# A two-layer hybrid encoder trunk on one Trainium2 core: the one-pass matrix products run their columns from the last to the first

## The chip, the core and the metric

The kernel runs on one core of one Trainium2 chip. The metric is the device time of one launch in microseconds (us), lower being better; a kernel's time is the median of its runs. TensorE does the matrix products (PE in the profile, and PEld for the loading of its stationary operand), VectorE is DVE, ScalarE is ACT, GpSimd is POOL, and SyncE (SP) issues most of the DMAs.

## The reference

Two layers over 512 tokens of width 1024. Layer 0 mixes the tokens by differential attention, layer 1 by chunk-causal gated linear attention; both also attend to 256 memory tokens, and each ends in a gated MLP with a causal convolution of width 3. Cut to what matters:

```python
for i in range(2):
    h = rms_norm(x, attn_norm[i])
    if i == 0:
        proj = h @ w_in_diff[0]                 # 512x1024 @ 1024x2560
        mix = diff_attention(q, k, v, ...)      # 6 heads, two maps of width 64 each
    else:
        proj = h @ w_in_gla[0]                  # 512x1024 @ 1024x2576
        mix = gla_attention(q, k, v, r, ...)    # 4 heads, chunks of 64
    cross = memory_cross_attention(mem_q, mem, mem_norm[i], w_mem_kv[i], mem_qk_norm[i])
    x = x + concatenate([mix, cross], -1) @ w_out[i]      # 512x1024 @ 1024x1024
    h = rms_norm(x, ffn_norm[i])
    u = h @ w_up[i]                             # 512x1024 @ 1024x5632
    a, g = split(causal_conv3(u) + conv_b[i])
    x = x + (silu(g) * a) @ w_down[i]           # 512x2816 @ 2816x1024
```

All inputs and outputs are float32.

## The kernel before

**A product in three one-pass terms.** TensorE takes operands of a rounded type (fp32r in the profile) in one pass. The kernel splits each float32 operand of a large product into a rounded high part and a rounded rest (`hi` and `lo`), and forms `hi*hi + hi*lo + lo*hi`: three matmuls, each with a stationary operand of 128x128 and a moving operand of 128 rows, added up in the same bank of PSUM. These are the one-pass products. A bank holds 512 float32 columns, and the moving operand and the output of a one-pass product are 512, 272 or 256 columns wide. The smaller products (the attention's scores and values, the transposes, the sums of squares) are of plain float32; each of them is recorded as two matmuls.

**Where they are issued.** There are four places.
- `gemm` (L327 to L329): the projections. The stationary operand is a block of 128 tokens of the activations, the moving one a row of weights; one bank collects eight row blocks of three terms.
- `product` (L348 to L350): the output projection and the MLP's up-projection. Here the weights are stationary and the activations (512 tokens) move.
- L507: the very first projection, written out by hand so that it starts while the inputs still arrive.
- `step` in `down` (L1173): the MLP's down-projection, done by a scheme of seven products of halves for each of its two column halves; the moving operand is 256 tokens wide, and two outputs of 256 columns share a bank.

One further pair of lines makes rounded products, the gates of layer 1 (L885); the change leaves it alone.

**What sets the order.** TensorE's instructions stand in the order in which they are written out. A queue of small pieces of work, `Filler`, holds the large products of the projections, and the attention code lets it run for so many microseconds between its own steps (`F.fill`), so that TensorE has products to do while VectorE and ScalarE work on a softmax. The banks come from a pool with two buffers for each of four names (`mm`, `sm`, `lg`, `tp`). Semaphore waits between the engines, and of an engine on itself, are put in by the framework from the regions that the instructions read and write.

**Who reads the banks.** ScalarE or VectorE takes a finished bank out, in ascending column order, once its last product has ended: L1178 for the down-projection, L1064 for the output projection, ScalarE's copies for the projections.

Of the kernel before, what the change touches and what calls it, by code (L numbers as in the profile page):

```python
# [22 lines left out]
KT = D // 128  # L23
# [127 lines left out]
def trunk(ctx, tc, head_d, x_t, mem_t, wpack, cols_a_d, cols_d, conv_d, gate_d, rel_bias, diff_lambda, consts, onehot, out):  # L151
    nc = tc.nc
    mm = nc.tensor.matmul
# [10 lines left out]
    def bank(tag):  # L164
        return ps.tile([128, 512], F32, name=f"ps_{tag}", tag=tag)

    def xtile():
        return xs.tile([128, S], F32, name="xt", tag="xs", bufs=XS)

    def pair(dt=F32):  # L170
        t = xs.tile([128, 2, S], dt, name="x2", tag="x2", bufs=X2)
        return t[:, 0], t[:, 1]
# [10 lines left out]
    def blk(b, w=128):  # L183
        return slice(w * b, w * b + w)
# [6 lines left out]
    eps = perm.tile([128, 1], F32, name="eps")  # L191
    V.memset(eps, EPS)

    def transpose(dst, src):
        n = src.shape[0]
        nc.tensor.transpose(dst, src, ident[:n, :n])  # L196
# [35 lines left out]
    def raw_tile():  # L232
        return wp.tile([128, WTILE], F32, name="raw", tag="raw", bufs=RAWS)

    def load_raw(raw, n):
        nc.sync.dma_start(raw[:, :n], wpack[at[0], :, :n])
        at[0] += 1
        return raw
# [57 lines left out]
    def weights(key, more=True):  # L296
        i = used[0]
        assert plan[i][0] == key, (plan[i][0], key)
        if more:
            prefetch(i)  # L300
        used[0] += 1
        parts, made[i] = made[i], None
        return parts
# [10 lines left out]
    def gemm(sh, sl, nb, key, w, evac, hook=None, order=None, hold=1):  # L314
        got, open_, held = [], {}, []
        order = order or [(b, "mm") for b in range(nb)]

        def unit(b, tag, k0, k1):
            if not got:
                for x in key if isinstance(key, list) else [key]:  # L320
                    got.extend(weights(x))
            if k0 == 0:
                open_[b] = bank(tag)[:, :w]
            p = open_[b]
            for k in range(k0, k1):
                hi, lo = got[k]
                mm(p, sh[k][:, blk(b)], hi, start=k == 0, stop=False)  # L327
                mm(p, sh[k][:, blk(b)], lo, start=False, stop=False)  # L328
                mm(p, sl[k][:, blk(b)], hi, start=False, stop=k == KT - 1)  # L329
            if k1 == KT:  # L330
                held.append(b)
                if len(held) < hold:
                    return
                if hook is not None and order[hold - 1][0] == b:
                    hook()
                for x in [x for x in held if x in open_]:
                    evac(x, open_.pop(x))
        for b, tag in order:
            for k in range(0, KT, 2):
                F.add(6 * w / 2370.0, lambda b=b, tag=tag, k=k: unit(b, tag, k, k + 2))  # L340


    def product(p, parts, n, pairs, ids=None):
        ids = range(len(parts)) if ids is None else ids
        first, last = (ids[0], ids[-1]) if len(ids) == len(parts) else (0, len(parts) - 1)
        for i in ids:
            (hi, lo), (bh, bl) = parts[i], pairs[i]
            mm(p, hi[:, blk(n)], bh, start=i == first, stop=False)  # L348
            mm(p, hi[:, blk(n)], bl, start=False, stop=False)  # L349
            mm(p, lo[:, blk(n)], bh, start=False, stop=i == last)  # L350


    xT, xpair = [None] * KT, [None] * (KT // 2)
# [56 lines left out]
    first = [bank("mm"), bank("mm"), bank("sm"), bank("sm")]  # L410
# [24 lines left out]
    with tc.tile_pool(name="ini", bufs=1) as ip, tc.manual_schedule(engines={E.Activation, E.DVE, E.Pool, E.SP}):  # L435
        idle = ip.tile([128, 512], F32, name="idle")
        rb = ip.tile([32, 6], F32, name="rb")
        oh = ip.tile([32, 640], F32, name="oh")
        bs = pair()
        bs = bs[0][:6], bs[1][:6, :128]  # L440
        lv = xtile()[:, :256]
        G.memset(idle, 0.0)
        p = bank("tp")
        for n in (512, 320):
            mm(p[:, :n], idle[:, 0:128], idle[:, :n], start=True, stop=True)


        raws = [ip.tile([128, WTILE], F32, name=f"raw{i}") for i in range(4)]
        A.dma_start(raws[0][:, blk(0, S)], wpack[0, :, blk(0, S)])
        head = ip.tile([128, 32 + S], F32, name="head")  # L450
        for c in (slice(0, 32 + S // 2), slice(32 + S // 2, 32 + S)):
            load(head[:, c], head_d[:, c])
        xT[0] = head[:, 32:]
        for k in range(1, KT):
            if k % 2:
                two = pair()
            xT[k] = two[1 - k % 2]
            load(xT[k], x_t[k])
            load(raws[k // 2][:, blk(k % 2, S)], wpack[k // 2, :, blk(k % 2, S)])
        load(cols_a, cols_a_d)  # L460
        at[0] = 4
        load(C[:, 640:768], consts[:, 640:768])
        load(rb, rel_bias)
        load(oh, onehot)
        second = [load_raw(raw_tile(), WTILE) for _ in range(3)]
        load(cols, cols_d)
        load(lv, diff_lambda[0].rearrange("a b -> (a b)").partition_broadcast(128))
        parts, acc, split_w = [], [None], [None]
        made.append(parts)

        def operands(k):
            if k % 2 == 0:
                split_w[0] = [wp.tile([128, WTILE], F32R, name=n, tag=n, bufs=WB) for n in ("whi", "wlo")]
            c = blk(k % 2, S)
            hi, lo = split_w[0]
            xh[k], xl[k] = split_tiles()
            if k == 0:
                V.tensor_copy(hi[:, c], raws[0][:, c])
                V.tensor_sub(lo[:, c], raws[0][:, c], hi[:, c].bitcast(F32))
                for t in (blk(0, S // 2), blk(1, S // 2)):  # L480
                    split(xh[0][:, t], xl[0][:, t], xT[0][:, t], col(0, head))
            else:
                split(xh[k], xl[k], xT[k], col(k, head))
                split_weights(c, raws[k // 2], hi, lo)
            parts.append((hi[:, c], lo[:, c]))
            squares(xT[k], acc)

        operands(0)
        for k in range(KT):
            if k + 1 < KT:  # L490
                operands(k + 1)
            if k == 0:
                second.append(load_raw(raws[0], WTILE))
            if k == 4:
                bias_rows(rb, oh, bs)
            if k == KT - 2:
                make_piece(second, lambda: token_rsqrt("lg", acc[0], NB, r_x[:, 0]))
                weights(("qk", 0))
                small_vectors()
                for c in range(2):  # L500
                    load(bias_d[:, 512 * c:min(512 * c + 512, 640)], bs[c])
            hi, lo = parts[k]
            terms = (xh[k], hi), (xh[k], lo), (xl[k], hi)
            todo = [(b, i) for b in range(NB) for i in range(3)]
            for b, i in sorted(todo, key=lambda bi: bi[1]) if k == 0 else todo:
                xp, w = terms[i]
                mm(first[b], xp[:, blk(b)], w, start=k == 0 and i == 0, stop=k == KT - 1 and i == 2)  # L507

    load(C[:, 0:640], consts[:, 0:640])
    for i in range(4):  # L510
# [595 lines left out]
    def ffn(pool, l, acc):  # L1106
# [47 lines left out]
        def down(g, mids, finish):  # L1154
            last, ks = len(mids) - 1, tuple(range(len(mids)))
            parts, banks, first, last_group = {}, {}, used[0], g + 1 == len(GROUPS)

            def step(c, tag, w, m, ks=ks, start=False, more=True):
                if (c, w) not in parts:
                    parts[c, w] = weights(("d", l, g, c, w), more)  # L1160
                elif more:
                    prefetch(first + more)
                if start:
                    banks[c, tag] = bank(tag)
                p = banks[c, tag]
                hi, lo = parts[c, w]
                for k in ks:
                    mh, ml = mids[k][m]
                    for n in range(2):
                        o, ws = p[:, blk(n, 256)], slice(256 * k + 128 * n, 256 * k + 128 * n + 128)  # L1170
                        terms = (hi, mh), (hi, ml), (lo, mh)
                        for i, (a, b) in enumerate(terms):
                            mm(o, a[:, ws], b, start=start and (k, n, i) == (0, 0, 0), stop=k == last and i == 2,  # L1173
                               skip_group_check=True)

            def add(c, tag, f, t):
# [89 lines left out]
        for what, i in _ffn():  # L1266
            if what == "up":
# [12 lines left out]
                if i % 2 == 0:  # L1280
                    w = pool.tile([128, 8, 256], F32, name="w", bufs=1)
# [3 lines left out]
            else:  # L1285
                n, last = GROUPS[i], i == len(GROUPS) - 1
# [93 lines left out]
```

## Time and profile before

| | |
|---|---|
| median of 3 runs | 1177.33 us (1175.06 to 1177.44) |
| the profiled execution | 1175.44 us |
| its span, first to last instruction | 1173.7 us |
| granted TensorE clock | 1.00 |
| PE busy | 1156.1 us, 6448 records |
| PEld busy | 988.8 us |
| DVE busy | 887.9 us |
| ACT busy | 599.1 us |
| POOL busy | 4.1 us |
| DMA | 117.94 MB, 100 GB/s |

"Busy" counts a stretch once however many instructions overlap in it. TensorE's matmuls overlap: the next one starts before the last columns of the one before have come out, so a matmul's own duration is longer than the distance to the next one's start. The pace of a chain is read from those distances in the timeline, and the duration minus the distance is the overlap.

### The profile page before, as it was taken

The numbers are of one execution on the slowest core, as the hardware profiler recorded it, in microseconds if no ns is written. First come the engines' busy times: TensorE is split into PE (matmuls) and PEld (weight loads), VectorE is DVE, ScalarE is ACT, GpSimd is POOL, SyncE is SP. The second block draws the span as 40 slices with busy tenths as digits, with TensorE's granted clock in tenths as the row PEclk, the third lists the DMA queues.
The fourth block names the chain that finished last, engine by engine and source line by source line (L and its number), as shares of the span: only waits on it lengthen the run. The fifth ranks groups of instructions, "written<-read, shape, count | busy, mean of one in ns | idle before, by whom it ended". The sixth has DMA issues, their size and how long they took to land.

```text
span 1173.7 us, 16700 instructions
## 1 busy us (share of the span) xinstructions
PE 1156.1 (99%) x6448; PEld 988.8 (84%) x6448; DVE 887.9 (76%) x1454; ACT 599.1 (51%) x1048; POOL 4.1 (0%) x17
## 2 busy tenths in 40 slices
PE   9999999999999999999999999999999999999998
PEld 6877776788899889988997788988789988998888
DVE  7747677779986778668897736868998777876885
ACT  6856676556444444344467534436654344434441
POOL 0000000000000000000000000000000000000000
PEclk9999999999999999999999999999999999999999
DMA  9532213243126222532253221144322632253211
GB/s 306 164 100 90 68 55 109 76 114 104 62 70 190 90 72 73 162 92 70 65 172 108 72 73 46 46 161 126 86 68 64 184 103 73 72 158 95 72 37 73
DMA packets 39277, 117.94 MB, mean 100 GB/s; under 512 B 4671, under 2 KB 6520, under 8 KB 39198
## 3 DMA queue, kind: packets, MB, share of 16 engines
q1 hardware_dynamic: 39054, 116.62, 31.8%
q8 instruction: 51, 0.84, 0.3%
q10 hardware_dynamic: 144, 0.26, 0.1%
q14 instruction: 28, 0.23, 0.1%
HBM read 112.65 MB, written 4.21 MB: 100 GB/s over the span
## 4 chain that ended last, share of the span: by engine, by line
PE 89%; DVE 6%; ACT 2%; DMA 1%; issue 1%; SPq 0%; DVEq 0%; ACTq 0%
PE ps_lg L1173 10%; PE ps_mm L349 8%; PE ps_mm L350 8%; PE ps_mm L348 8%; PE ps_sm L350 7%; PE ps_sm L349 7%; PE ps_sm L348 7%; PE ps_mm L327 5%; PE ps_mm L329 5%; PE ps_mm L328 5%; PE ps_tp L1173 5%; PE ps_mm L1173 3%; PE ps_tp L196 2%; PE ps_lg L686 1%; PE ps_sm L722 1%
## 5 line engine op out<-in xcount | busy, mean ns | idle before, releaser
L230 DVE TENSOR_TENSOR wlo<-raw,whi 128x1024 fp32r<-128x1024 f32 (+4 forms) x164 | 186.7, 1141 | 86.5 <-ACT whi L227 85.7
L227 ACT CAST whi<-raw 128x1024 fp32r<-128x1024 f32 (+4 forms) x164 | 160.7, 985 | 154.3 <-PE ps_sm L349 69.7
L348 PE MATMUL ps_mm<-x,whi 128*128 128x512 f32 x438 | 172.6, 394 | 0.4 <-DVE midh L1262 0.4
L349 PE MATMUL ps_mm<-x,whi 128*128 128x512 f32 x438 | 170.6, 389 | 0.2 <-DVE x L309 0.2
L350 PE MATMUL ps_mm<-x,wlo 128*128 128x512 f32 x438 | 170.6, 390 | 0.0
L348 PE MATMUL ps_sm<-x,whi 128*128 128x512 f32 x378 | 148.0, 392 | 0.0
L349 PE MATMUL ps_sm<-x,whi 128*128 128x512 f32 x378 | 147.1, 389 | 0.0
L350 PE MATMUL ps_sm<-x,wlo 128*128 128x512 f32 x378 | 147.1, 389 | 0.0
L327 PE MATMUL ps_mm<-whi,x 128*128 128x512 f32 (+2 forms) x336 | 132.0, 393 | 0.0
L329 PE MATMUL ps_mm<-whi,x 128*128 128x512 f32 (+2 forms) x336 | 126.6, 377 | 0.5 <-DVE x L309 0.4
L328 PE MATMUL ps_mm<-wlo,x 128*128 128x512 f32 (+2 forms) x336 | 126.1, 375 | 0.0
L263 ACT CAST whi<-raw 128x1024 fp32r<-128x1024 f32 (+1 forms) x60 | 58.3, 978 | 86.8 <-PE ps_sm L349 26.2
L348 PEld LDWEIGHTS ps_mm<-x,whi 128*128 128x128 f32 x438 | 82.2, 188 | 17.3 <-issue 0.9
L350 PEld LDWEIGHTS ps_mm<-x,wlo 128*128 128x128 f32 x438 | 82.2, 188 | 17.1
L349 PEld LDWEIGHTS ps_mm<-x,whi 128*128 128x128 f32 x438 | 82.3, 188 | 17.0 <-DVE x L309 0.6
L265 DVE TENSOR_TENSOR wlo<-raw,whi 128x1024 fp32r<-128x1024 f32 (+1 forms) x60 | 67.9, 1132 | 25.1 <-ACT whi L263 25.0
L349 PEld LDWEIGHTS ps_sm<-x,whi 128*128 128x128 f32 x378 | 71.0, 188 | 15.0 <-issue 0.5
L348 PEld LDWEIGHTS ps_sm<-x,whi 128*128 128x128 f32 x378 | 71.0, 188 | 15.0 <-issue 0.5
L350 PEld LDWEIGHTS ps_sm<-x,wlo 128*128 128x128 f32 x378 | 70.9, 188 | 14.7
L1173 PE MATMUL ps_lg<-midh,whi 128*128 128x256 f32 x264 | 74.9, 284 | 1.8 <-DVE x L1178 1.8
L1173 PE MATMUL ps_lg<-midh,wlo 128*128 128x256 f32 x264 | 74.7, 283 | 0.0
L1173 PE MATMUL ps_lg<-midl,whi 128*128 128x256 f32 x264 | 74.7, 283 | 0.0
(308 smaller groups left out, 2288.5 us busy)
## 6 DMA issues: line engine op xcount, KB each, us to landing
raw<-in_wpack_dram SPq DMA_DIRECT2D x170, 512.0 KB, 3.6
raw<-in_wpack_dram SPq DMA_DIRECT2D x24, 384.0 KB, 3.1
x<-in_x_t_dram SPq DMA_DIRECT2D x15, 256.0 KB, 4.1
xres<-x SPq DMA_DIRECT2D x8, 256.0 KB, 3.9
x<-xres SPq DMA_DIRECT2D x8, 256.0 KB, 4.7
out_dram<-x SPq DMA_DIRECT2D x8, 256.0 KB, 2.2
raw<-in_wpack_dram SPq DMA_DIRECT2D x7, 256.0 KB, 5.5
bt<-bias_d SPq DMA_DIRECT2D x6, 256.0 KB, 4.9
```

The lines of the kernel that those rows point to most:

```text
L196: nc.tensor.transpose(dst, src, ident[:n, :n])
L227: ins = A.copy(hi[:, c], raw[:, c])
L230: V.tensor_sub(lo[:, c], raw[:, c], hi[:, c].bitcast(F32))
L263: A.copy(hi[:, c], raw[:, c])
L265: todo = [lambda: V.tensor_sub(lo[:, c], raw[:, c], hi[:, c].bitcast(F32)), lambda: [sum_weights((*key[:3], *x)) for x in after]]
L327: mm(p, sh[k][:, blk(b)], hi, start=k == 0, stop=False)
L328: mm(p, sh[k][:, blk(b)], lo, start=False, stop=False)
L329: mm(p, sl[k][:, blk(b)], hi, start=False, stop=k == KT - 1)
L348: mm(p, hi[:, blk(n)], bh, start=i == first, stop=False)
L349: mm(p, hi[:, blk(n)], bl, start=False, stop=False)
L350: mm(p, lo[:, blk(n)], bh, start=False, stop=i == last)
L1173: mm(o, a[:, ws], b, start=start and (k, n, i) == (0, 0, 0), stop=k == last and i == 2, skip_group_check=True)
```

## The change

At all four places the moving operand and the output are given through a view with a step of -1: TensorE reads the moving operand's last column first and writes the output's last column first. The same numbers end in the same places. The stationary operands, the readers of the banks, the float32 products and the gates of layer 1 are as they were.

```diff
+    def back(t):
+        return t[:, ::-1]
+
...
-                mm(p, sh[k][:, blk(b)], hi, start=k == 0, stop=False)
-                mm(p, sh[k][:, blk(b)], lo, start=False, stop=False)
-                mm(p, sl[k][:, blk(b)], hi, start=False, stop=k == KT - 1)
+                mm(back(p), sh[k][:, blk(b)], back(hi), start=k == 0, stop=False)
+                mm(back(p), sh[k][:, blk(b)], back(lo), start=False, stop=False)
+                mm(back(p), sl[k][:, blk(b)], back(hi), start=False, stop=k == KT - 1)
...
-            mm(p, hi[:, blk(n)], bh, start=i == first, stop=False)
-            mm(p, hi[:, blk(n)], bl, start=False, stop=False)
-            mm(p, lo[:, blk(n)], bh, start=False, stop=i == last)
+            mm(back(p), hi[:, blk(n)], back(bh), start=i == first, stop=False)
+            mm(back(p), hi[:, blk(n)], back(bl), start=False, stop=False)
+            mm(back(p), lo[:, blk(n)], back(bh), start=False, stop=i == last)
...
-                mm(first[b], xp[:, blk(b)], w, start=k == 0 and i == 0, stop=k == KT - 1 and i == 2)
+                mm(back(first[b]), xp[:, blk(b)], back(w), start=k == 0 and i == 0, stop=k == KT - 1 and i == 2)
...
-                            mm(o, a[:, ws], b, start=start and (k, n, i) == (0, 0, 0), stop=k == last and i == 2,
+                            mm(back(o), a[:, ws], back(b), start=start and (k, n, i) == (0, 0, 0), stop=k == last and i == 2,
                                skip_group_check=True)
```

On every engine the instructions and their order stay the same. What moves is a number of waits of TensorE on its own semaphore (PE_49 below): 23 matmuls, each the first of its bank, have such a wait now and had none, and 7 that had one have none. One place is where the output projection of layer 0 opens a bank during the attention (`x_1240` is a half of the rounded mix of heads, `em` the attention's weights). Before:

```order
776 L722 MATMUL ps_sm<-v_388,em 128x128 x3
777 L348 MATMUL ps_mm<-x_1240,whi 128x512
778 L349 MATMUL ps_mm<-x_1240,whi 128x512
779 L350 MATMUL ps_mm<-x_1240,wlo 128x512
780 L196 MATMUL ps_tp<-C,em 128x128 [waits DVE_49,PE_49]
```

And now, with the lines three further down in the file:

```order
776 L725 MATMUL ps_sm<-v_388,em 128x128 x3
777 L351 MATMUL ps_mm<-x_1240,whi 128x512 [waits PE_49]
778 L352 MATMUL ps_mm<-x_1240,whi 128x512
779 L353 MATMUL ps_mm<-x_1240,wlo 128x512
780 L199 MATMUL ps_tp<-C,em 128x128 [waits DVE_49,PE_49]
```

The first product into the bank has gained the wait; the two that follow it into the same bank have none, and no instruction has changed its place.

## The prediction

> **What bounds the kernel now.** I read the page's busy rows first, then the waits of TensorE, then the chain, then the pace of the products in the timeline.
>
> ```profile
> PE 1156.1 (99%) x6448; PEld 988.8 (84%) x6448; DVE 887.9 (76%) x1454; ACT 599.1 (51%) x1048; POOL 4.1 (0%) x17
> PEclk9999999999999999999999999999999999999999
> PE 89%; DVE 6%; ACT 2%; DMA 1%; issue 1%; SPq 0%; DVEq 0%; ACTq 0%
> PE ps_tp L196 <- DVE qm L388: 2.8, 1, 2.8
> ```
>
> TensorE is busy in all but 17.6 us of a span of 1173.7 us (1173.7 - 1156.1), at its full clock in every slice; its longest single wait for another engine is 2.8 us. The chain that ended last is TensorE's work for 89%. So the time is the number of TensorE's products times the pace at which they follow each other, plus little. DVE, the next busiest, has 285 us of slack. Nothing that the change does reaches the other engines except through the moment at which a bank is finished.
>
> A busy TensorE need not run at its peak, so the pace itself is read from the timeline (start, duration, line). First the 512-wide one-pass products of `product`, 18 steps apart, then the 256-wide ones of the down-projection, 6 steps apart.
>
> ```profile
> 244.93 0.39 PE L348 MATMUL ps_mm<-mxh,whi 128*128 128x512 f32 x1
> ...
> 249.01 0.39 PE L348 MATMUL ps_mm<-x,whi 128*128 128x512 f32 x1
> ```
> ```profile
> 471.68 0.28 PE L1173 MATMUL ps_lg<-midh,whi 128*128 128x256 f32 x1
> ...
> 472.40 0.28 PE L1173 MATMUL ps_lg<-midh,whi 128*128 128x256 f32 x1
> ```
>
> 4.08 us over 18 steps is 226.7 ns for 512 columns; 0.72 us over 6 is 120.0 ns for 256. The difference, 106.7 ns for 256 columns, is 0.417 ns for a column, and what is left is a fixed part of 13.3 ns at either width. Each product lasts 0.39 us (or 0.28), so 163 ns of it overlap the next one (0.39 - 0.227, 0.28 - 0.12).
>
> How many there are comes from the busy time by source line (busy, count, for PE and then PEld; one row each for L348, L327, L507 and L1173) and from the groups that keep shapes apart.
>
> ```profile
> 0.00:1174.00 1174.00, 326.80 (x832) 156.23 (x832) 1.00 0.32 100
> 0.00:1174.00 1174.00, 136.66 (x352) 66.29 (x352) 1.00 0.32 100
> 0.00:1174.00 1174.00, 22.83 (x96) 18.00 (x96) 1.00 0.32 100
> 0.00:1174.00 1174.00, 223.35 (x1848) 222.68 (x1848) 1.00 0.32 100
> ```
> ```profile
> L327 PE MATMUL ps_mm<-whi,x 128*128 128x512 f32 x288 | 117.8, 409 | 0.0
> L327 PE MATMUL ps_mm<-whi,x 128*128 128x256 f32 x32 | 9.6, 301 | 0.0
> ```
>
> L348 has 832, and so have L349 and L350: 2496, all 512 wide. L327 to L329 have 3 x 352 = 1056: 864 of 512, 96 of 256, and the other 96 are 272 wide. L507 adds 96 of 512. So 3456 are 512 wide, and 1848 + 192 = 2040 are 256 or (96 of them) 272 wide; I count the latter as 256. At the paces above they fill 3456 x 226.7 ns + 2040 x 120 ns = 783 + 245 = 1028 us, 88% of the span. The change touches every one of these 5496, and nothing hides a nanosecond of them.
>
> **The change part by part.** The instructions and their order stay; three things could have a price.
>
> *Reading the moving operand backwards.* No TensorE row of before reads or writes with a negative step. The nearest row that reads backwards is VectorE's L691, which takes the attention's bias table with a step of -1; beside it stands a forward read of the same size:
>
> ```profile
> L691 DVE CUSTOM_DVE_ANT_0 em<-ps_lg,bt 128x512 f32<-128x512 f32 x12 | 8.0, 688 | 5.4 <-PE ps_lg L686 5.1 <-PE ps_sm L722 0.3
> L1178 DVE TENSOR_TENSOR x<-x,ps_lg 128x512 f32<-128x512 f32 x48 | 32.8, 684 | 10.0 <-PE ps_lg L1173 10.0
> ```
>
> 688 ns against 684 ns: backwards costs VectorE nothing. But it takes 1.34 ns for a column (688/512), while a one-pass product needs one every 0.417 ns, three times as fast. The row shows that the step is handled, not that it is handled at TensorE's one-pass pace.
>
> *Writing the output backwards.* Here there is not even a distant row: every writer of before goes upwards. What the trace does show is a slower pace at which the same TensorE reads and writes the same columns, the plain float32 products:
>
> ```profile
> 262.61 1.02 PE L1127 MATMUL ps_tp<-xt,C 128*128 128x512 f32 x2
> 702.82 1.14 PE L983 MATMUL ps_lg<-gv,kd 128*96 128x192 f32 x6
> ```
> ```profile
> L1127 PE MATMUL ps_tp<-xt,C x4: 592/592/593, 262.6 to 821.9; 128*128 128x512 f32 x4
> L983 PE MATMUL ps_lg<-gv,kd x24: 325/326/326, 702.8 to 774.9; 128*96 128x192 f32 x24
> ```
>
> Two 512-wide ones take 1.02 us and each lasts 592 ns, so they are 428 ns apart; six 192-wide ones take 1.14 us, so they are (1140 - 326)/5 = 163 ns apart. That is 0.83 ns for a column, twice 0.417, with a fixed part of about 3 ns. So TensorE has a full and a half pace for columns of four bytes, and a one-pass product runs at the full one. My estimate is that the full pace needs neighbouring columns to be taken and put two at a time in ascending order, and that a step of -1 drops the product to the half pace of these rows.
>
> The price of that: a 512-wide product goes from 226.7 to 512 x 0.834 + 3 = 430 ns if the fixed part falls to that of the float32 rows, and to 440 ns if it stays 13.3; a 256-wide one goes from 120 to 216.5 or 226.8 ns. By the first, 3456 x 203.3 ns + 2040 x 96.5 ns = 702.6 + 196.9 = 899.5 us; by the second, 3456 x 213.6 + 2040 x 106.8 = 738.2 + 217.9 = 956.1 us. Nothing in the rows tells which, so I take the middle, 928 us. The bounds of this part are nothing (L691) and 956 us, with more only in the last rival below; for a gain I see a reason only in the rival that names it.
>
> [...]
>
> *The new waits.* 23 first products of a bank now wait on TensorE's own semaphore. The dearest case is that a wait is for the product just ahead, which loses the overlap of 163 ns: 23 x 0.163 = 3.7 us. The cheapest is nothing: the framework adds a wait for the bank's former products, and those ended before ScalarE or VectorE emptied the bank, for which the new first product waits as it is. TensorE has some 55 such waits already, and none of them stands among its waits in the trace of before, whose longest entries are for other engines. I take nothing, and keep 0 to 3.7 us; the 7 waits that go are worth nothing either. While it waits, all of TensorE's queue stands behind it, and nobody else.
>
> The sum, against the profiled execution (1175.4 us, its span and 1.7 us around it; 0.16% below the median of the runs): 1175.4 + 928 + 0 = 2103 us. All of it lies on TensorE, which works in order. VectorE's 888 us and ScalarE's 599 us would spread over 2100 us and bind nowhere new; at most they shorten some of TensorE's 17.6 us of idle time. For this case alone the range is 1175.4 + 899.5 - 17.6 = 2057 to 1175.4 + 956.1 + 3.7 = 2135, rounded to 2055 to 2140.
>
> **The rivals.**
>
> *Direction is free.* [...] For it: L691 is as fast backwards as forwards, all rows start at a multiple of four columns and have an even width, so descending pairs are the same pairs as ascending ones. Against it: L691 is at a third of the pace. Then only the new waits are left: 1175.4 to 1179.1 us, not slower than can be told from no change, and this is the case on the other side of the forecast. It decides where the product keeps its 227 ns. With what runs differ by, 1173 to 1180. Chance 0.25.
>
> *A price for each product, not each column.* The start of a backward product costs more, at the fixed part of 13.3 ns or in the overlap of 163 ns. Another fixed part is 5496 x 13.3 ns = 73 us, so 1248 us; the loss of the whole overlap (the next product held until the former's columns are all in) is 5496 x 163 ns = 896 us, so 2071 us. For it: products into one bank follow each other column by column, and a check of that could know ascending order only. Against it: both products run in the same direction, so each column still has the same time between its two writes. Chance 0.14, anywhere between 1248 and 2071.
>
> *A gain.* The fixed part of 13.3 ns could come from the jump from the last column back to the first, and shrink to the 3 ns of the float32 rows: 5496 x 10.3 ns = 57 us, so 1119 us. Against it: a descending product jumps just as far, the other way, and the float32 rows jump too. Chance 0.07.
>
> *A quarter of the pace.* Each column is fetched alone and costs two of the half-pace steps, 1.67 ns: 3456 x 640 ns + 2040 x 320 ns = 2865 us more, 4040 us. No row of TensorE is that slow. Chance 0.07.
>
> **How the numbers follow.** The half pace has the remaining 0.47 and gives the time, 2103 us; its own range is 2055 to 2140. The range over the cases must hold 8 in 10: with the free direction (0.25), the price for each product (0.14) and the half pace (0.47) it holds 0.86, from 1173 to 2140; leaving out the free direction would leave out 0.39. About 0.2% (2.4 us) is what a measurement of this kernel can tell from no change. Within it lies the free direction but for 0.02 above (the waits at their dearest) and 0.01 below: same 0.22. Faster is the gain and that 0.01: 0.08. Slower is the rest: 0.70.
>
> **What would show each step.** In the profile of the changed kernel I look at the distance between starts of one-pass products: about 430 to 440 ns at 512 columns and 216 to 227 ns at 256 under the forecast, PE busy near 2080 us, durations up from 0.39 to about 0.6 us, and DVE's share of the span near 42%. The gates' products (L885, now L888), which stay forward and rounded, keep their durations. If the distances stay 227 and 120 ns, the step from slower rows to a backward one was wrong and direction is free. If the distances grow by the same amount at both widths, it is a price for each product: by 13 ns with durations as they were, or to the whole duration of 0.39 and 0.28 us. If only matmuls that open a bank show idle time ahead of them, with TensorE as its releaser, the waits cost what I took as nothing.

## The result and the profile after

| | before | after |
|---|---|---|
| median of 4 runs | 1177.38 us (1175.06 to 1177.49) | 1193.88 us (1192.13 to 1194.72) |
| ratio, 95% interval | | 1.0147 [1.0134, 1.0159] |
| the profiled execution | 1175.44 us | 1192.13 us |

The change costs 1.5%: far more than can be mistaken for no change, and less than a fiftieth of what was forecast. From the page of after (its span, the busy rows of the engines, the granted clock, the chain that ended last) and from TensorE's waits (for whom, us in all, times, longest):

```profile
span 1190.3 us, 16706 instructions
PE 1173.2 (99%) x6448; PEld 986.7 (83%) x6448; DVE 888.2 (75%) x1454; ACT 598.7 (50%) x1048; POOL 4.1 (0%) x17
PEclk9999999999999999999999999999999999999999
PE 88%; DVE 7%; ACT 2%; issue 1%; DMA 0%; DVEq 0%; ACTq 0%
PE ps_tp L199 <- DVE qm L391: 2.7, 1, 2.7
```

TensorE is busy for 17.1 us more (1173.2 - 1156.1) and the span is 16.6 us longer (1190.3 - 1173.7). The other engines do what they did, the granted clock stands in the top tenth in every slice (0.999 in the mean), and TensorE's longest wait is the one of before. So the time went into TensorE's own pace. The timeline of after shows it (start, duration): 18 steps of `product`, then 6 steps of the down-projection.

```profile
247.94 0.40 PE L351 MATMUL ps_mm<-x,whi 128*128 128x512 f32 x1
...
252.14 0.40 PE L351 MATMUL ps_mm<-x,whi 128*128 128x512 f32 x1
```
```profile
478.60 0.28 PE L1176 MATMUL ps_lg<-midh,whi 128*128 128x256 f32 x1
...
479.31 0.28 PE L1176 MATMUL ps_lg<-midh,whi 128*128 128x256 f32 x1
```

4.20 us over 18 steps is 233.3 ns, where before had 226.7: 6.6 ns more for each 512-wide product. 0.71 us over 6 is 118 ns, where before had 120: the 256-wide ones are a little faster. The busy time by source line (busy, count, for PE and then PEld; L351, then L1176) says the same of whole lines: 326.80 us became 333.44, and 223.35 became 220.77.

```profile
0.00:1191.00 1191.00, 333.44 (x832) 156.47 (x832) 1.00 0.32 99
0.00:1191.00 1191.00, 220.77 (x1848) 219.95 (x1848) 1.00 0.32 99
```

Adding up, over all TensorE's records of a place, the distance from each matmul's start to the next one's start gives the account of the whole change (worked out from the start times in the traces, us):

| place | records | before | after | read alone | write alone | 32 bytes before the weights |
|---|---|---|---|---|---|---|
| `product` | 2496 | 570.8 | 586.4 | 586.4 | 570.8 | 586.0 |
| `gemm` | 1056 | 233.4 | 236.8 | 237.5 | 233.7 | 236.6 |
| L507 | 96 | 23.0 | 22.8 | 23.3 | 23.8 | 23.2 |
| down step | 1848 | 224.0 | 222.0 | 221.9 | 224.0 | 223.4 |
| all else | 952 | 116.2 | 116.2 | 117.1 | 117.3 | 117.1 |

From before to after that is 15.6 + 3.4 - 0.2 - 2.0 = 16.8 us, all of the longer span. `product` pays 15.56 us / 2496 = 6.2 ns a matmul. (The entries are rounded; unrounded, the distances grow by 16.7 us and the span, 1173.65 to 1190.35 us, by 16.7 too.) The last three columns belong to experiments below.

### The profile page after: what moved, and what is told of

Read it like the earlier page. It is cut to its first block, busy times and chain, and to the rows that moved or that the text cites. A ratio compares the mean times of both kernels' runs of the same rounds, so it can differ in the third digit from the quotient of the medians.

```text
span 1190.3 us, 16706 instructions
## 1 busy us (share of the span) xinstructions
PE 1173.2 (99%) x6448; PEld 986.7 (83%) x6448; DVE 888.2 (75%) x1454; ACT 598.7 (50%) x1048; POOL 4.1 (0%) x17
## 4 chain that ended last, share of the span: by engine, by line
PE 88%; DVE 7%; ACT 2%; issue 1%; DMA 0%; DVEq 0%; ACTq 0%
PE ps_lg L1176 9%; PE ps_mm L352 8%; PE ps_mm L351 8%; PE ps_mm L353 8%; PE ps_sm L352 8%; PE ps_sm L353 8%; PE ps_sm L351 8%; PE ps_mm L330 5%; PE ps_mm L331 5%; PE ps_mm L332 5%; PE ps_tp L1176 4%; PE ps_mm L1176 2%; PE ps_tp L199 2%; PE ps_lg L689 1%; DVE wlo L268 1%
## 5 line engine op out<-in xcount | busy, mean ns | idle before, releaser
L351 PE MATMUL ps_mm<-x,whi 128*128 128x512 f32 x438 | 176.0, 402 | 0.1
L352 PE MATMUL ps_mm<-x,whi 128*128 128x512 f32 x438 | 174.2, 398 | 0.2 <-DVE x L312 0.2
L353 PE MATMUL ps_mm<-x,wlo 128*128 128x512 f32 x438 | 174.1, 397 | 0.0
L351 PE MATMUL ps_sm<-x,whi 128*128 128x512 f32 x378 | 151.1, 400 | 0.0
L353 PE MATMUL ps_sm<-x,wlo 128*128 128x512 f32 x378 | 150.2, 397 | 0.0
L352 PE MATMUL ps_sm<-x,whi 128*128 128x512 f32 x378 | 150.2, 397 | 0.0
L330 PE MATMUL ps_mm<-whi,x 128*128 128x512 f32 (+2 forms) x336 | 133.6, 398 | 0.0
L332 PE MATMUL ps_mm<-whi,x 128*128 128x512 f32 (+2 forms) x336 | 128.2, 382 | 0.5 <-DVE x L312 0.4
L351 PEld LDWEIGHTS ps_mm<-x,whi 128*128 128x128 f32 x438 | 82.4, 188 | 19.5 <-issue 0.6
L351 PEld LDWEIGHTS ps_sm<-x,whi 128*128 128x128 f32 x378 | 71.1, 188 | 17.2 <-issue 0.5
L1176 PE MATMUL ps_lg<-midh,whi 128*128 128x256 f32 x264 | 74.8, 284 | 2.3 <-DVE x L1181 2.3
L330 PEld LDWEIGHTS ps_mm<-whi,x 128*128 128x128 f32 x336 | 63.3, 188 | 14.4 <-issue 3.3
L332 PEld LDWEIGHTS ps_mm<-whi,x 128*128 128x128 f32 x336 | 63.2, 188 | 14.1 <-DVE x L312 1.0
```

What stands on the lines that cost most here:

```text
L330: mm(back(p), sh[k][:, blk(b)], back(hi), start=k == 0, stop=False)
L332: mm(back(p), sl[k][:, blk(b)], back(hi), start=False, stop=k == KT - 1)
L351: mm(back(p), hi[:, blk(n)], back(bh), start=i == first, stop=False)
L352: mm(back(p), hi[:, blk(n)], back(bl), start=False, stop=False)
L353: mm(back(p), lo[:, blk(n)], back(bh), start=False, stop=i == last)
L1176: mm(back(o), a[:, ws], back(b), start=start and (k, n, i) == (0, 0, 0), stop=k == last and i == 2, skip_group_check=True)
```

## The experiments

**The pace by itself.** The trunk is left out; chains of 48 one-pass products run into a bank, each with fresh weights, forward and backward, at several widths.

```python
def cols(t, w, how, o=0):
    if how == "b":
        return t[:, o:o + w][:, ::-1]
    if how == "s":
        return t[:, o:o + 2 * w:2]
    return t[:, o:o + w]
...
nc.tensor.matmul(cols(p[:m], w, o, oout), a[:, c:c + m], cols(b[:, n % 4], w, r, off), ...)
```

> This kernel leaves the trunk out and runs chains of 48 one-pass products each, all into one bank, at widths from 512 to 128 columns, with the moving operand read forward or backward and the output written forward or backward. The changed kernel's trace has 226.7 ns turned into 233.4 ns at 512 columns and 120.1 into 118.7 ns at 256. Theory R (the read is what costs): backward reading alone gives about 233 ns at 512, backward writing alone stays at 227. Theory W (the write is what costs): the other way round. Theory P (a price for each product that a slower weight load hides at 256 columns): the extra 6.7 ns is the same at 448, 384 and 320 columns, where the product is longer than the weight load, and with narrow weights of 32 columns it shows at 256 too. Theory C (a price for each column): the extra shrinks in proportion to the width, to 5 ns at 384 columns and 3.3 at 256 with narrow weights.

The timeline of this kernel (start, us for the whole chain). `wa` is 512 wide and `we` 256; `r` is the read and `w` the write, `f` forward and `b` backward; `rs` reads every second column; `offa` reads from one column later; `plain` is float32, two records each.

```profile
35.42 11.28 PE L181 MATMUL wa_rf_wf<-mv,st 128*128 128x512 f32 x48
46.54 11.28 PE L181 MATMUL wa_rf_wb<-mv,st 128*128 128x512 f32 x48
57.66 11.44 PE L181 MATMUL wa_rb_wf<-mv,st 128*128 128x512 f32 x48
68.94 11.44 PE L181 MATMUL wa_rb_wb<-mv,st 128*128 128x512 f32 x48
181.15 5.84 PE L181 MATMUL we_rf_wf<-mv,st 128*128 128x256 f32 x48
192.51 5.84 PE L181 MATMUL we_rb_wf<-mv,st 128*128 128x256 f32 x48
515.55 41.36 PE L181 MATMUL wa_plain_rf_wb<-raw,wraw 128*128 128x512 f32 x96
556.75 41.36 PE L181 MATMUL wa_plain_rb_wb<-raw,wraw 128*128 128x512 f32 x96
597.55 11.99 PE L181 MATMUL wa_offa_x<-mv,st 128*128 128x512 f32 x48
651.08 11.16 PE L181 MATMUL we_rs_wf<-mv,st 128*128 128x256 f32 x48
```

The pace is the total less one duration (0.39 to 0.40 us at 512, 0.28 at 256), divided by one less than the count. At 512 that is 231.6 ns for the forward read and 234.9 for the backward one, and which way the write goes changes nothing. At 256 it is 118.3 ns either way. Plain float32 takes 429 ns a record in all four directions, so its slowness has nothing to do with direction. There is no half pace for a step of -1. There is one for a step of 2: 229 ns at 256 columns.

Neither rule for the size of the extra held. Worked out in the same way, the backward read cost 3.3 ns more at 512 columns, 3.3 at 448, nothing at 384, 2.2 at 320 and nothing at 256; with weights of 32 columns it cost 2.5 ns at 512, and at 256 it was about half a nanosecond faster. That is neither the same price for each product nor one that shrinks in proportion to the width.

Two things did not fit a price of direction. The forward chain ran at 231.6 ns here and not at the kernel's 226.7, and a forward read that starts one column later (`offa`) took (11.99 - 0.41 - 0.63)/46 = 238 ns, once its first distance of 0.63 us is set aside: slower than backward. In this kernel the rows of the moving operand lie 520 columns apart, so they start at four different places. That suggested that the place at which a read starts counts.

**The read alone and the write alone.** One kernel reverses only the read, the other only the write, at all four places, so that the columns of each product come out mirrored; the second carries every self-wait that the change added. One line of each, first the read alone, then the write alone:

```diff
-            mm(p, hi[:, blk(n)], bh, start=i == first, stop=False)
+            mm(p, hi[:, blk(n)], back(bh), start=i == first, stop=False)
```
```diff
-            mm(p, hi[:, blk(n)], bh, start=i == first, stop=False)
+            mm(back(p), hi[:, blk(n)], bh, start=i == first, stop=False)
```

> All one-pass products read backward and write forward, so that the columns of each product come out mirrored; the amount of work is the same. Theory R: about 1193 us, as with both. Theory W: about 1177 us, as before. Theory S (the new waits of TensorE on itself, which come with the backward writes): about 1177 us.

> All one-pass products read forward and write backward, so that the columns come out mirrored. Theory R: about 1177 us. Theory W: about 1193 us. Theory S: about 1193 us with the 512-wide products still 227 ns apart and the time lost where banks are opened.

The read alone: 1194.32 us, a ratio of 1.0153 [1.0139, 1.0167]. The write alone: 1176.81 us, 1.0001 [0.9992, 1.0009]. The groups of the second line of `product` (busy, mean ns of one, idle before), first with the read reversed and then with the write:

```profile
L352 PE MATMUL ps_mm<-x,whi 128*128 128x512 f32 x438 | 174.2, 398 | 0.2 <-DVE x L312 0.2
```
```profile
L352 PE MATMUL ps_mm<-x,whi 128*128 128x512 f32 x438 | 170.6, 389 | 0.2 <-DVE x L312 0.2
```

The read lengthens a product from 389 to 398 ns; the write leaves it at 389. With the account above (`product` at 586.4 and 570.8 us), the whole cost is in the read, within that measurement's error: writing backward and the new waits together cost between -0.9 and +1.1 us (the interval times 1177 us).

**The down-projection alone.** Only the 256-wide products of the down step are reversed, read and write.

```diff
-                            mm(o, a[:, ws], b, start=start and (k, n, i) == (0, 0, 0), stop=k == last and i == 2,
+                            mm(back(o), a[:, ws], back(b), start=start and (k, n, i) == (0, 0, 0), stop=k == last and i == 2,
```

> Only the 256-wide products of the down-projection run backward, reading and writing. By the changed kernel's trace they follow each other at 118.7 instead of 120.1 ns: 1848 x 1.4 ns = 2.6 us faster, about 1174.8 us against 1177.4. If that pace came from something else in the changed kernel, 1177 us.

1174.94 us, 0.9982 [0.9973, 0.9991]: 2.0 us less than the 1176.95 of before on the same chip, as the 2.0 us of the account have it. The same edit has one sign at 512 columns and the other at 256, which again speaks against a price of direction.

**Where a read starts.** The trunk is left out again. Chains of 24 products, 512 wide unless a name says otherwise; the place of the moving operand's first column, or of the weights' first column, is moved.

```python
c = soff + 128 * (n % 8)
b = mv[:, n % 4, off:off + w]
nc.tensor.matmul(p[:m, :w], st[:, c:c + m], b[:, ::-1] if back else b, start=n == 0, stop=n == N - 1)
```

> This kernel leaves the trunk out and runs chains of 24 one-pass products whose moving operand starts k columns into its tile (k from 0 to 35 at 512 columns, every fourth at 256), read forward (fw) or backward (bw), and a few whose weights start k columns in. The tiles lie at the same address within 2048 bytes as the trunk's. Theory A (the address decides, not the direction): the forward pace varies with k and its values take in the backward ones; some forward start is as slow as the backward read at k = 0, which should show 233 ns against 227 forward, and some backward start is as fast as 227. Theory D (the direction decides): the forward chains stay near 227 to 231 ns at every k, the backward ones near 233 to 235.

From the timeline: `fw` is forward and `bw` backward with the moving operand 0 (`a`), 5 (`f`), 7 (`h`) or 8 (`i`) columns further on; `sfw_c` and `sbw_c` are forward and backward with the weights 8 columns further on. Then the durations of two of them, from the groups.

```profile
33.67 5.60 PE L175 MATMUL fw_a<-mv,st 128*128 128x512 f32 x24
61.43 5.92 PE L175 MATMUL fw_f<-mv,st 128*128 128x512 f32 x24
72.79 5.60 PE L175 MATMUL fw_h<-mv,st 128*128 128x512 f32 x24
78.23 5.76 PE L175 MATMUL fw_i<-mv,st 128*128 128x512 f32 x24
234.66 5.76 PE L175 MATMUL bw_a<-mv,st 128*128 128x512 f32 x24
500.40 5.75 PE L175 MATMUL sfw_c<-mv,st 128*128 128x512 f32 x24
506.00 5.76 PE L175 MATMUL sbw_c<-mv,st 128*128 128x512 f32 x24
```
```profile
L175 PE MATMUL fw_a<-mv,st 128*128 128x512 f32 x24 | 5.6, 389 | 0.0
L175 PE MATMUL bw_a<-mv,st 128*128 128x512 f32 x24 | 5.8, 397 | 0.0
```

`fw_a` has both operands at the same place, as the kernel before has (a place is where a read starts within a stretch of 512 bytes, the size of a block of weights; the chains' tiles were laid out like the kernel's): (5.60 - 0.389)/23 = 226.6 ns. `bw_a`, the same read backward, has 233.2: the 226.7 and 233.3 of the two kernels. But a forward read pays as much or more as soon as it starts elsewhere (233 ns at 8 columns, 240 at 5), or as soon as only the weights start elsewhere (`sfw_c`, 233 ns). Over the 36 starts tried, the first four distances of each chain left out, forward reads took 226.6 to 240.0 ns, 232.7 in the mean, and backward ones 233.3 to 242.3, 235.2 in the mean. So over all starts the two directions differ by 2.5 ns in the mean, and the kernel before lies at a place where forward is at its best. One half of the expectation missed: no backward start was as fast as 227. With the chains in which the weights moved, 42 backward ones were run, and none was below 233 ns.

**Moving the tiles in the kernel, forward.** If that is right, the kernel before must slow down without any reversal. One version puts 32 unused bytes ahead of the weights' tiles; the control puts them ahead of all tiles, so that every distance between operands stays. The version, then the control:

```diff
+    wp.tile([128, 8], F32, name="pad", bufs=1)
```
```diff
+    perm.tile([128, 8], F32, name="pad")
```

> The kernel before, all products forward; an unused tile of 32 bytes ahead of the weights' tiles moves them, and the MLP's middle tiles with them, by 8 columns against the activations' tiles, which stay. Theory A (the place of the two operands against each other sets the pace; 227 ns is a lucky place, which the backward read leaves): the 512-wide products go from 227 to 233 ns without any backward read, as the chains with weights or moving operand 8 columns further showed (232.9 and 233.5 ns), and the time rises to about 1193 us. Theory D (only the direction costs): 1177 us, as before.

> The kernel before, with the unused tile of 32 bytes ahead of all tiles, so that weights and activations move together. If only their place against each other counts: 1177 us. [...] Theory D: 1177 us.

With the weights moved: 1194.29 us, 1.0150 [1.0137, 1.0163]. With everything moved: 1176.77 us, 0.9998 [0.9990, 1.0007]. Thirty-two bytes of nothing cost what the reversal cost, and almost wholly in the same places (the account's last column: `product` 15.2 us, `gemm` 3.2). The timeline of the first has a control within itself: `mxh` and `mxl`, the mix of heads, lie behind the weights and moved with them, and `x` did not.

```profile
247.09 0.39 PE L350 MATMUL ps_mm<-mxh,whi 128*128 128x512 f32 x1
...
247.77 0.40 PE L350 MATMUL ps_mm<-x,whi 128*128 128x512 f32 x1
...
248.47 0.40 PE L350 MATMUL ps_mm<-x,whi 128*128 128x512 f32 x1
```

Three products that read the mix take 0.68 us, 227 ns each; the next three, which read `x`, take 0.70 us, 233 ns each. Same weights, same direction. Over all 48 products of the mix the mean is 229.3 ns, against 227.2 before the move, with some of the first of each group at up to 236; the products of `x` have 233.3, against 226.9.

**Both operands moved, and 256 columns.** The same chains with other places.

```python
for k in (4, 8, 12, 16, 24, 28, 32):
    run(f"both_{L[k]}", 512, False, k, k)
    run(f"hboth_{L[k]}", 256, False, k, k)
```

> Chains of products alone, forward only: 256 columns with the moving operand 0 to 63 columns into its tile, 512 columns at 36 to 63, moving operand and weights shifted by the same number of columns, and weights alone shifted at 256 columns. Theory A: the shifts by the same number keep 226.7 and 120.0 ns, and the pace at 256 ranges between about 113 and 124 ns over the starts; there are starts with less than 120 ns that the down-projection could use. Theory D: all within 1 ns.

From the timeline: `both_bq` has both operands moved by 8 columns; `hw` is 256 wide with the moving operand 0 (`aq`) and 48 (`gq`) columns further on; `sh_cq` is 256 wide with the weights 16 columns further on.

```profile
381.42 5.62 PE L175 MATMUL both_bq<-mv,st 128*128 128x512 f32 x24
33.61 3.04 PE L175 MATMUL hw_aq<-mv,st 128*128 128x256 f32 x24
170.76 2.90 PE L175 MATMUL hw_gq<-mv,st 128*128 128x256 f32 x24
440.16 2.89 PE L175 MATMUL sh_cq<-mv,st 128*128 128x256 f32 x24
```

Moved together by 8 columns the two keep about 227 ns ((5.62 - 0.39)/23). By 16, 24 and 32 columns they settle at 226.7 too, after at most eight products with distances of up to 236; by 4, 12 or 28 columns they stay at 231.1. So of the seven moves of both that were run, the four by whole multiples of 8 columns (32 bytes) came back to 226.7 or about 227 ns, and the other three did not: the distance between the two reads counts, but not alone. At 256 columns the same place for both, 120 ns, is not the best: 113.3 ns is to be had by moving either operand ((2.90 - 0.28)/23 = 114 from the rounded row), and that led to the next version.

**A version that is faster.** Forward again, with 192 unused bytes ahead of the MLP's tiles, so that its rounded mid tiles `midh` and `midl` start 48 columns further on than the weights.

```diff
     def ffn(pool, l, acc):
+        pool.tile([128, 48], F32, name="pad", bufs=1)
         rB = xtile()
```

> The kernel before, all products forward; an unused tile of 192 bytes (48 columns) at the head of the MLP's pool moves the middle tiles, the moving operand of 10 of the 14 steps of the down-projection, against the weights. Theory A: at 48 columns the chains alone ran at 113.3 instead of 120.0 ns at 256 columns, so 1320 of the 1848 products of 256 columns gain 6.7 ns each: 8.8 us, about 1168 us. Theory D: 1177 us.

1170.78 us, 0.9949 [0.9935, 0.9962]: 6.1 us better than the 1176.92 of before. The timeline, the busy time of the down step's line, and TensorE's wait for the additions of the down step:

```profile
470.59 0.28 PE L1174 MATMUL ps_lg<-midh,whi 128*128 128x256 f32 x1
...
471.95 0.28 PE L1174 MATMUL ps_lg<-midh,whi 128*128 128x256 f32 x1
```
```profile
0.00:1170.00 1170.00, 215.88 (x1848) 214.80 (x1848) 1.00 0.31 101
PE ps_lg L1174 <- DVE x L1179: 3.3, 3, 1.2
```

12 steps take 1.36 us, 113.3 ns each instead of 120. The sum of the distances of the down step falls from 224.0 to 218.2 us, 5.8 of the 6.1. Expected were 8.8. Within a bank the products gain 7.4 us (212.5 to 205.1); of that, the wait for the additions, now reached sooner, takes 1.5 back (1.8 us before, 3.3 now).

**The reversal on moved tiles.** If backward reads do not have the good place, the reversed kernel must not care for the 32 bytes ahead of the weights.

```diff
+    wp.tile([128, 8], F32, name="pad", bufs=1)
```

> The changed kernel with the unused tile of 32 bytes ahead of the weights' tiles that made the forward kernel 17 us slower. Theory A with what the chains showed (backward at 512 columns was 233.3 ns at each of six starts of the weights): about 1194 us, as the changed kernel without the tile; the backward read has no 227 ns to lose. If the backward read and the shift add up: about 1211 us. If the shift gives the backward read its place back: about 1177 us.

1193.50 us against before, 1.0144 [1.0130, 1.0158], where the reversed kernel itself has 1.0147. From the timeline, 9 steps, products of the mix and of `x` among them:

```profile
249.26 0.40 PE L353 MATMUL ps_mm<-x,whi 128*128 128x512 f32 x1
...
251.36 0.40 PE L353 MATMUL ps_mm<-x,whi 128*128 128x512 f32 x1
```

2.10 us over 9 is 233.3 ns for both. Reversal and displacement do not add up: each of them only takes the good place away.

**What stays open.** That the two reads share something is argued from the chains in which only the weights moved; what it is, no run shows. A smaller load of weights did not help: with weights of 32 columns, at the kernel's own place, a forward chain took 231.5 ns, and at seven other starts 230.1 to 233.4. Every one-pass product that was run loads fresh weights (6448 loads for 6448 matmuls in the kernel before, 3168 for 3168 in the first chains), so no run shows whether the place counts without that load. Nor do the runs show why 233.3 ns is the best that a backward read reached at any of the places, why the best place at 256 columns is another one than at 512, or why `gemm`'s 512-wide products, with another pair of tiles in the two roles, averaged 229.0 ns before (233.6 after).

## Why the prediction was wrong, step by step

**What bounds the kernel** held. The other engines hid none of it: 16.7 us of distances became 16.7 us of span.

**Reading backward** is the step that failed: "the full pace needs neighbouring columns to be taken and put two at a time in ascending order, and that a step of -1 drops the product to the half pace". The 512-wide product went from 226.7 to 233.3 ns, not to 430 or 440. The term of 928 us measured 16.7. The estimate took a price from rows that are slow for another reason: plain float32 keeps its 429 ns whichever way it is read or written. Those rows showed that a slower pace exists, not that direction leads to it, and the one row of a backward read, L691 with 688 against 684 ns, pointed the other way and was set aside for its slower pace. That columns go two at a time was an estimate from 0.83 ns a column being twice 0.417, and no run shows it.

The half pace does exist for another read: every second column, 229 ns at 256 columns against 118.

**Writing backward**, for which there was no row, costs nothing: 1.0001 [0.9992, 1.0009], and equal chains to the last digit.

**The new waits** at nothing were right; the write alone carries them all, and their dearest case of 3.7 us lies outside its interval (-0.9 to +1.1 us).

**The rivals.** *Direction is free* was true of the write. For the read it named the right test (whether the distances stay 227 and 120 ns), and the test went against it: 233.3 and 118. *A price for each product, not each column* came nearest: the distance and the duration both grow (226.7 to 233.3, 389 to 398 ns). But its term was mis-sized, 13.3 ns where `product` paid 6.2 and the down step gained 1.1 (2.0 us over 1848), so 16.7 us instead of 73. And its reason fell: the price belongs to the place from which a product reads, and a forward product pays it too once 32 bytes move it (1.0150, the products of `x` at 233.3 ns). Reversing costs at a good place, because no backward read reached that pace (none of 42 chains was below 233 ns); at the places of the 32-byte version it cost nothing more (1.0144 against 1.0150). *A gain* from a smaller fixed part came true only for the down step, 2.0 us of the 57. *A quarter of the pace* did not occur.

The measured 1194 us lies inside the stated 1173 to 2140 by luck: that range runs from one case to the next, and no case gave a time between 1180 and 1248.

**What none of the cases had** is that the pace of before was not the pace of a forward read, but of a forward read at one favourable place. The 13.3 ns of "fixed part" was taken as a constant of the engine; it is 13.3 at this layout, and, with 0.417 ns a column kept, between 13.2 and 26.6 elsewhere at 512 columns (226.6 to 240.0 less 213.4) and down to 6.6 at 256 (113.3 less 106.7).

## What to carry to other kernels

Before pricing a step by a slower row, ask whether that row is slow for the reason that the step brings in; if only the existence of a slower pace is known, the step needs a row of its own. In a kernel bound by back-to-back one-pass products, treat the place where the moving tile starts against the weights' tile as a parameter: a few unused bytes ahead of one pool are worth trying, for each width by itself, and an edit that shifts tiles can change the time without changing an instruction (here by +1.5% with 32 bytes ahead of the weights and by -0.5% with 192 bytes ahead of the MLP's tiles). A regression of that size after a harmless edit is then checked with a pad before the edit is blamed.

## What the hardware did that was not expected

- 32 unused bytes ahead of the weights cost 1.5% (1.0150), and 192 unused bytes ahead of the MLP's tiles gain 0.5% (0.9949), with the same instructions.
- A one-pass product with the same operands takes 226.6 to 240.0 ns at 512 columns by where its read starts, and moving only the weights changes it from 226.6 to 233 ns.
- The direction of the write changes nothing that can be measured (1.0001), nor does that of the read for plain float32 (429 ns a record); reading every second column halves the pace (229 against 118 ns at 256 columns).
